# A reordered start for an RMSNorm and projection kernel: other order of loads, two K blocks of weights first, two tiles transposed by DMA

## Chip, cores, metric

One core of a Trainium2 chip. The metric is the device time of one execution in microseconds, median of several; the profile gives a span some 2 us shorter.

## The reference, cut

```python
# x [8, 1024, 768] f32, gamma [768], w_qkv [768, 2304] f32 -> out [8, 1024, 2304] f32
rms = np.sqrt(np.mean(x ** 2, axis=-1, keepdims=True) + eps)
return np.matmul(x / rms * gamma, w_qkv)
```

8192 rows are 64 tiles of 128. K = 768 is six blocks of 128; N = 2304 is four blocks of 512 columns and one of 256. So each tile needs 30 matmuls.

## The kernel before

The weights are loaded in pieces and scaled by gamma into bf16. Rows are normalised last: the eviction multiplies by 1/rms. While the weights arrive, six tiles are worked on at once by a written plan of times (the **head**); 58 tiles follow by a formula. The times only sort the instructions. Each engine then runs its own in order.

```python
ARRIVALS = "xxxwwwxwwwwwxxwww"      # order of the loads on the SP queue
PIECES = [(0, 1, 0, 512), ..., (0, 6, 2048, 256)]   # K blocks k0..k1, columns n0..n0+n
HEAD_PLAN = [(4.41, "trA", 0), (4.45, "stat", 0), ..., (8.02, "mm", 0, 0, "0"), ...]
# [cut] tr: transposes on TensorE; cp: copy PSUM -> SBUF; conv: scaling of a weight block
    def trans_dma(t):
        XT[t] = xTp.tile([P, KO, P], bf16, name="xT")
        nc.sync.dma_start_transpose(out=XT[t], in_=XB[t])
# [cut] idle: matmuls on zeros, meant to keep the TensorE clock up
    def idle(n):
        wps = psum.tile([P, P], f32, name="pm")
        for _ in range(n):
            nc.tensor.matmul(out=wps, lhsT=warm, rhs=warm, start=True, stop=True)
# [cut] after the head
    for t in range(HEAD, MT):
        at(now - 15, load_x, t)
        at(now - 8.5, cast, t)
        at(now - 7.5, trans_dma, t)
        at(now - 5, stat, t)
        at(now - 3, recip, t)
        for n0 in range(0, N, NT):
            at(now, mm, t, n0, range(KO))
            now += min(NT, N - n0) * US
            flip ^= 1
            evac_at(now + 0.2, t, n0, "DVE" if flip else "ACT", gap=1.2)
```

All loads, stores and DMA transposes go through the SP queue, at most eight in flight.

## Time and profile before

| | before |
|---|---|
| device time, median (runs) | 389.93 us (3) |
| span of the profile | 387.9 us |
| TensorE busy | 98% |
| first matmul | 8.48 us |
| first matmul of tile 7 | 51.56 us |
| last matmul ends | 384.35 us |

Columns: start us, us, what.

```profile
384.35 0.02 issue
384.37 0.47 ACT ot L232
```

From 384.35 to 387.9 are 3.55 us of last eviction, last store and program end.

### The profile page before, as it was taken

The page shows a single profiled execution, that of the slowest core. Times are in us where ns is not written, and L with a number is a line of the kernel's source. Part 1 is how long each engine was busy: PE and PEld are TensorE (multiplying, and loading weights), DVE is VectorE, ACT ScalarE, POOL GpSimd, SP SyncE. Part 2 cuts the span into 40 slices and gives each one's busy share as a digit, 9 for nine tenths or more (in the row PEclk, how much of TensorE's full clock was granted, in tenths as well). Part 3 has the DMA queues.
Part 4 walks back from the last instruction along what each step waited for, and adds up shares of the span by engine and source line. Part 5 has one row for each costly group of instructions (what it writes and reads, how often), then busy time and mean ns, then how long its engine had stood idle before and what let it go on. Part 6 is the DMA issues. An engine that isn't in the chain of part 4 may idle for free.

```text
span 387.9 us, 5500 instructions
## 1 busy us (share of the span) xinstructions
PE 379.5 (98%) x1953; PEld 194.3 (50%) x1992; DVE 159.1 (41%) x317; ACT 178.1 (46%) x359; POOL 5.9 (2%) x12
## 2 busy tenths in 40 slices
PE   7999999999999999999999999999999999999996
PEld 6444644554554554554554554554554554554553
DVE  3667634343433343433343433343334343334332
ACT  6652234544444544444534444534434535434532
POOL 1310000000000000000000000000000000000000
PEclk9999999999999999999999999999999999999999
DMA  7999999999999999999999999999999999999974
GB/s 272 392 384 358 308 369 284 397 301 274 333 311 305 279 326 295 290 330 300 276 346 288 302 317 280 318 311 304 287 318 301 297 318 303 287 325 292 292 264 189
DMA packets 87606, 119.51 MB, mean 308 GB/s; under 512 B 50710, under 2 KB 59676, under 8 KB 87580
## 3 DMA queue, kind: packets, MB, share of 16 engines
q1 hardware_dynamic: 87568, 119.17, 100.7%
q8 instruction: 15, 0.25, 0.3%
q14 instruction: 11, 0.09, 0.1%
q10 hardware_dynamic: 12, 0.00, 0.0%
HBM read 32.25 MB, written 75.50 MB: 278 GB/s over the span
## 4 chain that ended last, share of the span: by engine, by line
PE 94%; DMA 3%; SPq 1%; issue 1%; DVE 0%; ACT 0%
PE pm L216 94%; DMA w_f<-in_w_qkv_dram 2%; DMA xT<-xb 2%; SPq L140 0%; SPq L145 0%; PE pm L183 0%; DVE w_b L151 0%; ACT ot L232 0%; DVE ot L230 0%
## 5 line engine op out<-in xcount | busy, mean ns | idle before, releaser
L216 PE MATMUL pm<-w_b,xT 128*128 128x512 bf16 (+1 forms) x1881 | 372.4, 357 | 3.0 <-DMA xT<-xb 0.4
L216 PEld LDWEIGHTS <-xT 128*128 128x128 bf16 x1920 | 187.6, 98 | 186.6 <-issue 0.8
L230 DVE TENSOR_SCALAR ot<-pm,rstd 128x512 f32<-128x512 f32 (+1 forms) x168 | 116.7, 696 | 210.3 <-PE pm L216 210.3
L232 ACT ACTIVATE ot<-pm,rstd 128x512 f32<-128x512 f32 (+1 forms) x152 | 97.9, 645 | 187.0 <-PE pm L216 141.7
L170 ACT ACTIVATE sq<-x_t 128x768 bf16<-128x768 f32 x64 | 53.4, 834 | 10.2 <-DMA x_t<-in_x_dram 10.2
L159 DVE CAST xb<-x_t 128x768 bf16<-128x768 f32 x61 | 33.2, 545 | 4.1 <-DMA x_t<-in_x_dram 4.0
L172 ACT ACTIVATE rms<-ssq,eps_sb 128x1 f32<-128x1 f32 x64 | 18.8, 294 | 2.1
L170 ACT ACTIVATION_READ_ACCUMULATOR sq<-x_t 128x1 f32 x64 | 12.2, 191 | 0.0
L177 DVE RECIPROCAL rstd<-rms 128x1 f32<-128x1 f32 x64 | 9.8, 153 | 0.0
L151 DVE TENSOR_SCALAR w_b<-w_f,g_sb 128x512 bf16<-128x512 f32 (+1 forms) x14 | 6.5, 494 | 6.1 <-DMA w_f<-in_w_qkv_dram 6.0
L153 ACT ACTIVATE w_b<-w_f,g_sb 128x512 bf16<-128x512 f32 (+1 forms) x10 | 6.1, 651 | 5.7 <-DMA w_f<-in_w_qkv_dram 5.7
L155 POOL TENSOR_SCALAR w_b<-w_f,g_sb 128x512 bf16<-128x512 f32 (+1 forms) x6 | 5.2, 864 | 23.5 <-DMA w_f<-in_w_qkv_dram 23.5
L265 PE MATMUL pm<-warm 128*128 128x128 bf16 x35 | 3.8, 300 | 1.0 <-DVE eps_sb L124 1.0
L265 PEld LDWEIGHTS <-warm 128*128 128x128 bf16 x35 | 3.5, 142 | 1.0 <-DVE eps_sb L124 1.0
L197 PE MATMUL pm<-ident_f,x_t 128*128 128x128 f32 x18 | 2.8, 292 | 0.8 <-DMA x_t<-in_x_dram 0.8
L197 PEld LDWEIGHTS pm<-ident_f,x_t 128*128 128x128 f32 x18 | 2.2, 155 | 1.1 <-DMA x_t<-in_x_dram 1.0
L127 ACT ACT_TABLE_LOAD x1 | 1.3, 1283 | 1.3 <-PEq L325 1.3
L159 DVE CAST xT<-pm 128x512 bf16<-128x512 f32 (+1 forms) x3 | 1.7, 596 | 0.0
L159 DVE COPY xT<-pm 128x768 bf16<-128x768 bf16 x3 | 1.6, 547 | 0.0
L248 DVE COPY g_sb<-pm 128x6 f32<-128x6 f32 x1 | 0.2, 165 | 3.6 <-PE pm L247 3.6
L183 PEld LDWEIGHTS <-xb 128*128 128x128 bf16 x18 | 1.2, 98 | 0.9 <-DVE xb L159 0.6
L183 PE MATMUL pm<-ident,xb 128*128 128x128 bf16 x18 | 1.5, 220 | 0.0
(13 smaller groups left out, 3.1 us busy)
## 6 DMA issues: line engine op xcount, KB each, us to landing
out_dram<-ot SPq DMA_DIRECT2D x126, 512.0 KB, 4.0
x_t<-in_x_dram SPq DMA_DIRECT2D x64, 384.0 KB, 4.3
out_dram<-ot SPq DMA_DIRECT2D x64, 128.0 KB, 3.2
w_f<-in_w_qkv_dram SPq DMA_DIRECT2D x2, 1536.0 KB, 13.3
w_f<-in_w_qkv_dram SPq DMA_DIRECT2D x3, 768.0 KB, 8.5
w_f<-in_w_qkv_dram SPq DMA_DIRECT2D x6, 256.0 KB, 5.8
out_dram<-ot SPq DMA_DIRECT2D x4, 256.0 KB, 2.0
xT<-xb SPq DMA_TRANSPOSE x58, 4.4
```

Of the source, the lines that this page charges most:

```text
L151: nc.vector.tensor_scalar(out=o, in0=i, scalar1=g, scalar2=None, op0=mult)
L153: nc.scalar.activation(out=o, in_=i, func=AF.Copy, scale=g, bias=0.0)
L155: nc.gpsimd.tensor_scalar(out=o, in0=i, scalar1=g, scalar2=1.0, op0=mult, op1=mult)
L159: nc.vector.tensor_copy(out=out, in_=in_)
L170: nc.scalar.activation(out=sq, in_=X[t], func=AF.Square, accum_out=ssq)
L172: nc.scalar.activation(out=rms, in_=ssq, func=AF.Sqrt, scale=inv_k, bias=eps_sb)
L177: nc.vector.reciprocal(out=r, in_=RS[t])
L197: nc.tensor.transpose(out=PT[t, h][:, ko - k0, :], in_=X[t][:, ko * P:(ko + 1) * P], identity=ident_f)
L216: nc.tensor.matmul(out=PM[t, n0][:, :nl], lhsT=XT[t][:, ko, :], rhs=w_b[:, ko, n0:n0 + nl], start=(b == 1), stop=(b == KO))
L230: nc.vector.tensor_scalar(out=o, in0=pm[:, :nl], scalar1=RS[t], scalar2=None, op0=mult)
L232: nc.scalar.activation(out=o, in_=pm[:, :nl], func=AF.Copy, scale=RS[t], bias=0.0)
L265: nc.tensor.matmul(out=wps, lhsT=warm, rhs=warm, start=True, stop=True)
```

## The change

The intent: start with two K blocks of weights, order the head by a list schedule chosen for late landings, and take the transposes of tiles 4 and 5 off TensorE.

```diff
-ARRIVALS = "xxxwwwxwwwwwxxwww"
-PIECES = [(0, 1, 0, 512), (1, 2, 0, 512), ...]
+PIECES = [(0, 2, 0, 512), (2, 3, 0, 512), ..., (0, 3, 1024, 512), (3, 6, 1024, 512), ...]
+LOADS = [
+    (-9.00, "w", 0), (-8.99, "x", 0), (-8.98, "x", 1), (-8.97, "x", 2), (-8.96, "w", 1),
     ...
+    (16.69, "t", 4), (16.70, "w", 9), (21.71, "t", 5), (21.72, "w", 10), (21.73, "w", 11),
+    (21.74, "x", 6), (21.75, "x", 7),
+]
 HEAD_PLAN = [   # all times and the order are new
 ...
-    at(0.0, idle, 30)
+    at(0.0, idle, 18)
+    at(2.8, gamma_in)
+    at(2.81, idle, 28)
 ...
-            evac_at(time, *args, gap=1.0)
+            evac_at(time, *args, gap=max(1.0, LOADS[-1][0] + 0.1 - time))
 ...
     for t in range(HEAD, MT):
-        at(now - 15, load_x, t)
-        at(now - 8.5, cast, t)
-        at(now - 7.5, trans_dma, t)
+        ahead = 6.0 if t < HEAD + 5 else 0.0
+        if ("x", t) not in {q[1:] for q in LOADS}:
+            at(now - 15 - ahead, load_x, t)
+        at(now - 8.5 - ahead, cast, t)
+        at(now - 7.5 - ahead, xbar, t)
```

Cut: more buffers (10, 6 and 11 for x, its bf16 copy and its transpose, before 8, 4 and 9), and at most four for each form of weight piece. The stores of the head now wait behind the last loads.

## The prediction

> **What bounds the kernel now.** I read the page first, then the chain of waits, then the waits of TensorE alone, then the timeline of the first 60 us.
>
> ```profile
> PE 379.5 (98%) x1953; PEld 194.3 (50%) x1992; DVE 159.1 (41%) x317; ACT 178.1 (46%) x359; POOL 5.9 (2%) x12
> ...
> PE 94%; DMA 3%; SPq 1%; issue 1%; DVE 0%; ACT 0%
> ```
>
> TensorE is busy for 98% of the span, and 94% of the chain that ended last is its matmuls. What is left to win is the start, before the first matmul, and the holes after it. The waits of TensorE in the whole run, after the opening:
>
> ```profile
> PE pm L216 <- DMA xT<-xb: 0.4, 1, 0.4
> PE pm L216 <- POOL w_b L155: 0.4, 1, 0.4
> PE pm L216 <- DVE w_b L151: 0.2, 1, 0.2
> ```
>
> Columns: total us, times, longest. About 1 us of waits in 388. Now the chain from 4 to 62 us (start us, us, what):
>
> ```profile
> 10.64 0.50 DVE w_b L151
> 11.14 0.04 issue
> 11.19 6.80 PE pm L216 x30
> 17.99 0.34 PE pm L183 x6
> 18.32 0.26 PE pm L216
> 18.58 0.05 issue
> 18.63 0.38 PE pm L216
> 19.01 0.34 PE pm L183 x6
> ...
> 45.30 0.02 issue
> 45.33 0.15 DVE ot L230
> 45.48 6.04 DMA xT<-xb
> 51.52 0.05 issue
> 51.56 6.22 PE pm L216 x31
> ```
>
> The reader is to see three things. The head (six row tiles while the weights arrive) ends at 45.3. Each TensorE transpose of a tile costs 0.34 us in it. Tile 7 waits at 51.56 for its crossbar transpose, issued only at 45.48 because the DMA queue stood behind stores. From 51.56 the matmuls run to 384.35: 57 tiles (7 to 63) in 332.8 us, 5.838 us a tile.
>
> So the head before is: first matmul at 8.48 (timeline), 6 x 5.838 = 35.03 of matmuls, 3 x 0.34 = 1.02 of transposes (tiles 3, 4, 5), 0.43 of holes between 8.48 and 11.19 (2.71 less nine matmuls at 0.216 and one transpose). Sum 44.96; the trace says 45.30, so 0.34 is small change that I carry over as 0.3.
>
> **What the Trainium skill says.** (1) "TensorE: Matmul & The Clock Gate", part 1: a warm matmul of N columns takes N / 2.4 GHz plus some 2.5 ns, 215.7 ns for 512. A tile is 24 of 512 and 6 of 256 columns: 24 x 0.2157 + 6 x 0.109 = 5.83 us. The trace agrees with 5.838: no matmul can be made faster here. (2) "DMA: Bandwidth & Descriptors", on why a semaphore goes up by 16: a transfer has landed only when the last of its 16 engines has. (3) "Runtime: NRT & Kernel Launch", instruction fetch mechanics: instructions come in blocks of 16 KiB (256 instructions) over a DMA, mostly hidden. Together they matter. DMA of 17.5 to 18.6 us:
>
> ```profile
> q1 hardware_dynamic: 206, 0.42, 103.1%
> q8 instruction: 1, 0.02, 6.2%
> ```
>
> 6.2% of 16 engines over 1.1 us is 1.1 us of one engine, on which every later piece queues. The piece behind it (the first six-block one, 7.08 MB into the stream) is due at 22.1 by the rate below and was seen at 23.18:
>
> ```profile
> 23.18 0.88 DVE L151 TENSOR_SCALAR w_b<-w_f,g_sb 128x512 bf16<-128x512 f32 x2 [1.88 <-DMA w_f<-in_w_qkv_dram]
> ```
>
> So the trace shows a fetch that is not hidden when loads are late. (4) "PSUM — Partial Sum Buffer", four rules: eight banks, one output at most one bank. The kernel has all eight in one ring, so an eviction may be late by up to seven outputs.
>
> **The change part by part.** Landing line, from the trace: 2.62 MB were in at 10.64, 5.11 MB at 17.03, 0.39 MB/us; other amounts by that line. An x tile is 0.393 MB, a K block of 512 columns 0.262.
>
> *The start.* The two-block piece goes first, so the third x tile has 1.70 MB ahead of and in it instead of 1.18, and lands at 8.3 (before, 1.70 MB was the second weight piece, used at 8.32) against 6.9. In the new TensorE order all six transposes of tile 2 stand before the first matmul. Six took 0.88. First matmul at 9.2 against 8.48: **+0.7**. In return four matmuls are ready at once; the next piece (1.97 MB, 9.0, plus a scaling of 0.49) is ready at 9.5 when they end at 10.06. Following the order to the fourth tile (48 matmuls, one transpose) I find no hole: pieces due at 11.3, 12.0, 14.0, 16.0 are scaled 0.4 us or more before use. The holes of 0.43 are gone: **-0.4**.
>
> *Transposes.* Tiles 4 and 5 leave TensorE: 2 x 0.34 = **-0.7**.
>
> Head without stalls: 9.2 + 35.03 + 0.34 + 0.3 = 44.9, against 45.3.
>
> *New waits.* After 48 matmuls TensorE is at 9.2 + 10.36 + 0.34 = 19.9 and wants the piece at 5.90 MB, due at 19.05, scaled by 19.55. But the change runs 49 idle matmuls instead of 35 and leaves out 12 transposes before this point: the fetch comes after about as many instructions, now some 33 matmuls into the head (16.8) and not 41 (18.5). It then hits this piece: 20.15, scaled 20.65, a stall of 0.7. Sixteen matmuls on (23.4, or 24.1) comes tile 4, which wants its crossbar transpose. That stands in the queue behind the x tile at 7.08 MB (22.1, or 23.2 with the late engine); its 768 packets of 256 B took 0.8 to 2.2 us in the undisturbed transposes of the trace. It lands at 23.3 to 25. Stall 0 to 1. I put the two stalls at **+0.9** together (0.1 without the fetch, 1.7 at worst). Head end 45.8.
>
> *Tiles 6 and 7.* Their loads now come before all stores and their casts and transposes 6 us earlier. The wait at 51.56 goes: **-0.4**. Against it, stores of the head start about 6 us later and pile up. Until tile 8's transpose (wanted near 57) the queue must move about 17.8 MB at 0.4 MB/us and five transposes: near 56.5. A wait of some tenths is possible: **+0.1**.
>
> Sum: +0.7 - 0.4 - 0.7 + 0.9 - 0.4 + 0.1 = +0.2, less rounding. From 389.93: **390.0 us**. The other 56 tiles and the end don't change.
>
> **Rivals.** *A: the stalls don't come* (the fetch falls elsewhere, the crossbar transpose is quick). For it: the list schedule puts tile 4 just after that landing, and was made for late landings. Then head end 44.9 to 45.0 and no wait at tile 7: 389.1. *B: VectorE blocks.* The cast of tile 6 is placed by a fixed formula before the evictions of tile 5, and its x lands only behind the last weights, at about 34. VectorE stands still for 3 to 4 us there, and again at the casts of tiles 8 to 10. For it: the engine is in order. Against: the eviction held up (tile 5, first column block) is done by 35.7 and its bank is wanted eight outputs later, at about 37. If x is 2 us later, TensorE stalls too: 391 to 392. *C: the delayed stores starve tiles 8 to 10* of transposes: up to 1 us each, 391 to 392. *D: hidden anyway*: the head is bound by arrivals, so that the order doesn't matter. Against: nearly all of TensorE's head from 11.19 is gapless, so removed transposes do count.
>
> **Range and chances.** A gives 389.1, the sum 390.0, B or C 391 to 392; I give A 30%, the sum half, B and C together 20%. Range 389.1 to 391.2. Two per cent is 7.8 us: more than the whole of holes, transposes and start that can be won after the first x tile (1.0 + 1.0 + some 4), and a loss of that size needs B and C several times over. Same 0.985, slower 0.01, faster 0.005.
>
> **What would show it.** First matmul at 9.2 (8.5 would be a win I don't expect). Six transposes on the bf16 transpose line instead of 18, none between 17.9 and 19.4. Two waits of TensorE near 20 and 24, the first on a scaled weight, the second on a crossbar transpose; the instruction block in the DMA view near 17. End of the head at 45.8. No wait at tile 7. VectorE idle for 3 us or more before the cast of tile 6, without a wait of TensorE behind it. The prediction is wrong if TensorE has waits on evictions, or waits of over 1 us on transposes after tile 6, or if the first matmul is before 8.7.

## The result and the profile after

| | before | after |
|---|---|---|
| device time, median (4 runs each) | 390.01 us | 389.32 us |
| span of the profile | 387.9 us | 387.4 us |
| first matmul | 8.48 us | 8.71 us |
| last matmul ends | 384.35 us | 383.38 us |
| last matmul to end of span | 3.55 us | 4.0 us |

The ratio is 0.9984, interval 0.9966 to 1.0001. A ratio is the mean of one kernel's runs over the mean of the other's in the same rounds, so it is not quite the ratio of these medians. The forecast of 390.0 with a range of 389.1 to 391.2 held, and so did "same".

The waits of TensorE after the change (total us, times, longest); apart from those of the opening there is this one:

```profile
PE pm L229 <- DVE w_b L164: 0.6, 1, 0.6
```

The chain in order of time:

```profile
19.56 0.02 issue
19.59 0.50 DVE w_b L164
20.08 0.04 issue
20.12 363.25 PE pm L229 x1872
383.38 0.02 issue
383.40 0.47 ACT ot L245
```

The reader is to see that from 20.12 on TensorE never stops: no wait for tile 4's transpose, none at tile 7. At the steady rate the head then ends at 20.12 + 96 x 0.2158 + 36 x 0.109 = 44.8. The trace's last matmul is 0.97 us earlier, the span only 0.5.

The timeline around the one wait, and the DMA view of 14.5 to 15.5 us:

```profile
17.54 0.56 DVE L172 CAST xb<-x_t 128x768 bf16<-128x768 f32 x1 [1.39 <-DMA x_t<-in_x_dram]
19.59 0.88 DVE L164 TENSOR_SCALAR w_b<-w_f,g_sb 128x512 bf16<-128x512 f32 x2 [0.59 <-DMA w_f<-in_w_qkv_dram]
```

```profile
q1 hardware_dynamic: 152, 0.38, 98.7%
q8 instruction: 1, 0.02, 6.8%
```

One instruction block, 6.8% of 16 engines over 1.0 us: 1.09 us of one engine. It came at 14.6 us, not at 16.8. The x tile after it and the weight piece after that, the one I named, are late. (In five later profiles it is the piece before; see below.)

Why the start cost less than the forecast 0.7 us is in the stretches of 5 to 6.5 and 6.5 to 18 us (last column GB/s), first before, then after:

```profile
5.00:6.50 1.50, 1.14 (x9) 0.88 (x9) 1.35 (x4) 0.48 (x2) 0.00 (x0) 1.00 0.87 247
6.50:18.00 11.50, 10.46 (x59) 5.21 (x61) 6.52 (x16) 7.76 (x17) 3.56 (x4) 1.00 1.04 388
```

```profile
5.00:6.50 1.50, 1.50 (x19) 1.50 (x17) 0.48 (x1) 1.28 (x2) 0.00 (x0) 1.00 1.05 412
6.50:18.00 11.50, 11.38 (x67) 6.03 (x66) 6.85 (x16) 8.64 (x20) 3.33 (x4) 1.00 1.04 390
```

The DMA had a slow stretch when the first weights came. With the weights first, it falls earlier, into the ramp (205 and 279 GB/s in the half microseconds from 2.5 and 3.0, where before had 406). By 8 us, 2.15 MB were moved and not 1.99, which is 0.4 us. A second pair of profiles has the same slow stretches (249 GB/s, and 176 and 299). That the first weight rows are slow is my reading of their packets; no run isolates it.

### The profile page after: what moved, and what is told of

Its sections match the earlier page's. It is cut to its first block, busy times and chain, and to the rows that moved or that the text cites. A ratio compares the mean times of both kernels' runs of the same rounds, so it can differ in the third digit from the quotient of the medians.

```text
span 387.4 us, 5550 instructions
## 1 busy us (share of the span) xinstructions
PE 381.7 (99%) x1994; PEld 195.0 (50%) x1994; DVE 153.7 (40%) x309; ACT 181.2 (47%) x362; POOL 7.5 (2%) x15
## 4 chain that ended last, share of the span: by engine, by line
PE 94%; DMA 4%; SPq 0%; DVE 0%; ACT 0%; issue 0%
PE pm L229 94%; DMA w_f<-in_w_qkv_dram 4%; SPq L153 0%; DVE w_b L164 0%; ACT ot L245 0%; SPq L158 0%
## 5 line engine op out<-in xcount | busy, mean ns | idle before, releaser
L243 DVE TENSOR_SCALAR ot<-pm,rstd 128x512 f32<-128x512 f32 (+1 forms) x165 | 113.6, 693 | 201.0 <-PE pm L229 200.7
L245 ACT ACTIVATE ot<-pm,rstd 128x512 f32<-128x512 f32 (+1 forms) x155 | 100.2, 648 | 190.6 <-PE pm L229 143.9
L185 ACT ACTIVATE rms<-ssq,eps_sb 128x1 f32<-128x1 f32 x64 | 18.9, 295 | 2.1
L168 POOL TENSOR_SCALAR w_b<-w_f,g_sb 128x512 bf16<-128x512 f32 (+1 forms) x9 | 6.8, 765 | 24.3 <-DMA w_f<-in_w_qkv_dram 16.2
L164 DVE TENSOR_SCALAR w_b<-w_f,g_sb 128x512 bf16<-128x512 f32 (+1 forms) x12 | 5.2, 449 | 3.9 <-DMA w_f<-in_w_qkv_dram 3.9
L278 PE MATMUL pm<-warm 128*128 128x128 bf16 x49 | 5.4, 301 | 1.0 <-DVE eps_sb L137 1.0
L278 PEld LDWEIGHTS <-warm 128*128 128x128 bf16 x49 | 4.9, 142 | 1.0 <-DVE eps_sb L137 1.0
L174 ACT CAST xT<-pm 128x256 bf16<-128x256 f32 (+1 forms) x3 | 1.2, 445 | 0.3 <-PE pm L210 0.2
L174 ACT COPY xT<-pm 128x768 bf16<-128x768 bf16 x1 | 0.8, 799 | 0.3 <-PE pm L196 0.3
L196 PEld LDWEIGHTS <-xb 128*128 128x128 bf16 x6 | 0.4, 98 | 0.2
```

The costliest lines, as they stand in the source:

```text
L164: nc.vector.tensor_scalar(out=o, in0=i, scalar1=g, scalar2=None, op0=mult)
L168: nc.gpsimd.tensor_scalar(out=o, in0=i, scalar1=g, scalar2=1.0, op0=mult, op1=mult)
L185: nc.scalar.activation(out=rms, in_=ssq, func=AF.Sqrt, scale=inv_k, bias=eps_sb)
L243: nc.vector.tensor_scalar(out=o, in0=pm[:, :nl], scalar1=RS[t], scalar2=None, op0=mult)
L245: nc.scalar.activation(out=o, in_=pm[:, :nl], func=AF.Copy, scale=RS[t], bias=0.0)
```

## The experiments

Theory: the gain is the transposes taken off TensorE (P), plus the wait before tile 7 taken away by early loads (T), less a wait that TensorE's own instruction fetch makes (F). Rivals: the transposes were hidden (H); the late piece is late for the queue's order (Q); the wait at tile 7 was no matter of the queue (N).

Runs of one series share the runs of the kernel before. Its medians were 390.53 (11 runs), 389.81 (9), 389.95 (9) and 390.25 (9) in the four series; compare within a series.

### The changed kernel again (series 1)

> The changed kernel again, as the yardstick of this series. Every theory: first matmul 8.7 us, one wait of 0.5 to 0.6 us for a scaled weight near 20.1, no wait for a transpose, last matmul at 383.4, time 0.6 to 0.8 us under the kernel before. The time from the last matmul to the end of the span was 3.5 before and 4.0 after in the first profiles: if that is the end of the program as such it is again 4.0, if it is chance it differs.

Median 389.39 (5 runs), ratio 0.9971, interval 0.9959 to 0.9983. Waits of 0.5 and 0.2 for scaled weights, last matmul at 383.50, again 4.0 us to the end of the span. The block hit one piece earlier here:

```profile
16.84 0.98 POOL L168 TENSOR_SCALAR w_b<-w_f,g_sb 128x512 bf16<-128x512 f32 x1 [1.66 <-DMA w_f<-in_w_qkv_dram]
```

That piece was used at 15.72 in the first profile. So which piece is late varies with the moment, and a loss stays: 0.56 there, 0.69 here. The longer end is no chance.

Four more profiles below keep the 49 narrow idle matmuls (both with transposes put back, the one without early loads, the one with more slots). In all four the waits are where they are here, at 17.2 to 17.4 and 17.8 to 18.0; with this one they add up to 0.30 to 0.75 us.

### Wide idle matmuls (series 1)

```diff
-    at(0.0, idle, 18)
+    at(0.0, idle, 4)       # each 512 columns wide, not 128
-    at(2.81, idle, 28)
+    at(2.81, idle, 6)
-    (7.26, "idle", 3)
+    (7.26, "idle", 1)
```

> The 49 narrow idle matmuls become 11 of 512 columns: about the same time, 76 instructions fewer on TensorE. Theory F (TensorE's instruction block of 16 KB is fetched after a count of instructions and holds up one DMA engine, and through it the piece wanted at 19.6): the fetch moves from about 14.9 us to about 22.6 to 23, the first piece of the third column block is used at 18.7 and not 19.59, the 0.56 us wait goes, last matmul near 382.8, time 0.5 us under the changed kernel. Rival Q (the piece is late for the order of the queue or the rate of the memory): it is used at 19.5 to 19.6 as before and the wait stays.

Median 389.23 (5), ratio 0.9966, interval 0.9954 to 0.9978. The block of 14.6 us is gone from its place and stands in the DMA view of 23 to 24 us; the piece is used at 18.51, and no wait is left in the head:

```profile
q8 instruction: 1, 0.02, 6.6%
```

```profile
18.51 0.88 DVE L164 TENSOR_SCALAR w_b<-w_f,g_sb 128x512 bf16<-128x512 f32 x2 [0.57 <-DMA w_f<-in_w_qkv_dram]
```

F holds, Q falls: the queue's order is the same, only the count of TensorE instructions is not. In thirteen of the fourteen profiles the first block came after 204 to 218 TensorE instructions, at times from 14.3 to 24.0 us; in the next run it came after 186. But the last matmul, at 383.28, was not near 382.8. A new wait took the gain:

```profile
68.64 1.90 SPq L219 DMA_TRANSPOSE xT<-xb  x1
73.84 1.47 PE L229 MATMUL pm<-w_b,xT 128*128 128x512 bf16 x6 [0.62 <-DMA xT<-xb]
```

This is tile 11, the first whose transpose isn't early. I had not foreseen it. In the changed kernel this transpose landed at 73.42 and TensorE reached tile 11 at 73.95. Here TensorE was there at 73.2, and the transpose landed at 73.79, 0.37 later: the faster head makes part of the wait, the later landing the rest.

### Fewer wide idle matmuls taken away (series 1): a test that missed

```diff
-    at(0.0, idle, 18)
+    at(0.0, idle, 5)       # 512 columns
-    at(2.81, idle, 28)
+    at(2.81, idle, 11)
```

> 17 wide idle matmuls, 64 instructions fewer than the changed kernel. Theory F: the fetch falls at about 21 us, onto the last x tile or the crossbar transpose of tile 4 behind it; the weight piece is on time (18.7), the wait near 20 goes, and in its place TensorE waits 0.3 to 0.8 us for the transpose of tile 4 near 23; time as the changed kernel within 0.3 us. Rival Q: the wait near 20 stays at 0.5 to 0.6, none near 23.

Median 389.92 (6), ratio 0.9986. My count of idle time was wrong: the 11 took 4.22 us, TensorE began its transposes at 7.8 and the first matmul came at 9.94. The fetch fell at 20.4 and made the last x tile of the head 1 us late, as F says (22.48, against 21.53 in the run before). But TensorE, 1.2 us behind, didn't have to wait for anything. So the wait for tile 4's transpose that I expected was not tested. What follows is something else: a start 1.2 us later moved the last matmul by 0.5 only (383.89), because it swallowed the waits.

### Transposes of tiles 4 and 5 back on TensorE (series 1 and 2)

```diff
-    (16.69, "t", 4), ... (21.71, "t", 5),
+    (22.82, "tr", 4), (22.83, "cp", 4, "DVE"), (22.84, "mm", 4, 0, "012345"),
+    (28.43, "tr", 5), (28.44, "cp", 5, "DVE"), (28.45, "mm", 5, 0, "012345"),
```

> Tiles 4 and 5 are transposed by TensorE again, right before their first matmul, and not by the crossbar; all else as in the changed kernel. Theory P (TensorE's head is gapless there, so its transposes are paid in full): 2 x 0.34 us, plus up to 0.3 us for the copy to SBUF that the matmuls then wait for; last matmul at 384.1 to 384.6, time 0.7 to 1.2 us over the changed kernel. Rival H (the head is bound by arrivals, the transposes were hidden): within 0.2 us of the changed kernel.

Median 391.56 (5), ratio 1.0025; last matmul at 385.83, 2.3 us later than the changed kernel of this series. More than half of it is my placement: TensorE waited 1.3 us for the two copies.

```profile
PE pm L229 <- DVE xT L172: 1.3, 2, 0.7
```

So I placed them better:

```diff
+    (21.95, "tr", 4), (21.96, "cp", 4, "DVE"), (21.97, "mm", 0, 1024, "34"), (21.97, "cast", 5, "DVE"),
+    (27.13, "tr", 5), (27.14, "cp", 5, "DVE"), (27.15, "mm", 3, 1024, "345"),
```

> Tiles 4 and 5 transposed by TensorE again, each transpose now placed ahead of matmuls that don't need it, so that the copy is hidden (in the last run TensorE waited 0.65 us twice for the copy). Theory P (transposes in TensorE's head are paid in full): 2 x 0.34 = 0.7 us over the changed kernel, last matmul at 384.0 to 384.3. Rival H (hidden behind arrivals): last matmul at 383.3 to 383.6.

Median 389.69 (5), ratio 0.9992. The copies are hidden; the chain has the transposes in TensorE's gapless stretch:

```profile
17.80 5.12 PE pm L229 x23
22.92 0.34 PE pm L196 x6
23.25 5.18 PE pm L229 x24
28.43 0.34 PE pm L196 x6
28.77 355.32 PE pm L229 x1836
```

Last matmul at 384.09, 0.6 to 0.7 later than the two profiles of the changed kernel. P holds, H falls: 0.34 each, paid in full; where the copy wasn't covered, in the run before, each wait of TensorE came on top (0.65 on average).

### The kernel before, profiled again (series 2)

No edit.

> The kernel before as a run of its own, for a second profile: in the last series its times spread over 2 us (389.3 to 391.3), those of the changed kernel over 0.5. Theory L (it has waits for crossbar transposes and late pieces whose length is chance): the profile shows waits of TensorE of 0.8 us or more, with the one before tile 7 of another length than 0.44. Rival: the waits are the same to 0.1 us and the spread lies outside the core's span.

Median 389.76 (5). Its chain:

```profile
19.56 25.88 PE pm L216 x138
45.44 5.92 DMA xT<-xb
```

Tile 7 begins at 51.40; tile 6 would end at 45.44 + 5.84 = 51.28. The wait is 0.12 here and was 0.44: chance sets its length. The first matmul waited 0.8 for GpSimd and not 0.4. The end is 3.55 again. The spread of 2 us that the kernel before had in series 1 I didn't catch in a profile; it lies within the span (387.5 to 388.7 us for two of those runs), and its cause stays open.

### Without the early loads, and the early loads alone (series 2)

```diff
-    (21.74, "x", 6), (21.75, "x", 7),
-        ahead = 6.0 if t < HEAD + 5 else 0.0
+        ahead = 0.0
```

> The changed kernel with the loads, casts and transposes of tiles 6 to 10 at their old times. Theory T (the early ones took away the wait before tile 7): TensorE waits for a transpose at tile 6 or 7 again, 0.3 to 1.2 us in all, last matmul at 383.8 to 384.6. Rival N (the wait at tile 7 was not from the order of the queue): no such wait, last matmul at 383.4.

Median 394.65 (4), ratio 1.0123, interval 1.0106 to 1.0141: far more than either theory said.

```profile
PE pm L228 <- DMA xT<-xb: 3.9, 1, 3.9
```

```profile
50.00:55.00 5.00, 1.14 (x9) 0.62 (x8) 1.61 (x3) 1.92 (x4) 0.00 (x0) 1.00 1.09 312
55.00:60.00 5.00, 5.00 (x17) 1.94 (x16) 0.70 (x2) 0.69 (x1) 0.00 (x0) 0.66 1.08 320
```

In the second line the clock column (last but two) falls to 0.66 after TensorE stood still for 3.9 us; the trace has half speed from 55.10 to 58.52. That costs another 5 x 0.34 = 1.7 us. The Trainium skill has this in "TensorE: Matmul & The Clock Gate", part 1 (the clock halves after an idle window of some 3.4 us); the trace agrees. So T holds with a turn: in the changed kernel the early loads are not only worth 0.4. They pay for the stores that were moved behind the loads.

Then the kernel before, with the early part alone:

```diff
+        ahead = 6.0 if t < HEAD + 5 else 0.0
-        at(now - 15, load_x, t)
+        at(-7.2 + 0.01 * t if t < HEAD + 2 else now - 15 - ahead, load_x, t)
         # cast and transpose ahead too; more buffers
```

> The kernel before, with only the early loads, casts and transposes of tiles 6 to 10 and the buffers for them. Theory T: no wait before tile 7, 0.4 us gained or somewhat more, last matmul at 383.8 to 384.0, and a smaller spread of the times. Rival N: the wait stays or turns up at a later tile, last matmul at 384.3 or later.

Median 389.39 (5), ratio 0.9986, interval 0.9973 to 0.9998. No wait from 19.64 to the end, last matmul at 384.03 against 384.19 and 384.35. N falls. By the last matmul the early part is worth 0.16 to 0.32 of the 0.97; counted from the last transpose of the head, which ended at 19.64 here and at 19.56 and 19.34 in the two profiles of before, 0.24 to 0.62.

### The end, and a version that beats both (series 3 and 4)

In the expectations that follow, the end "after the last written byte" is counted from a time set 0.24 us late: 1.14, 1.40 and 1.59 there are 1.38, 1.63 and 1.83 on the clock of the span. The 2.8 to 3.0 and 2.4 from last matmul to last byte hold the same 0.24. Differences aren't touched by it. SP waits at the end for each of its eight slots in turn, and the changed kernel has three DMAs more. With the order of the kernel before, the slot of the last store is the last one waited for. In the changed kernel it is among the first: SP sees this store at 385.95, and the waits for the other slots that follow last until 386.56, though those stores are long done. That is 0.6 us in all five profiles of this order.

```diff
+        if 40 <= t < 45:      # two halves: five DMAs more, last store in the old slot
+            nc.sync.dma_start(out=X[t][:, :K // 2], in_=xf[t * P:(t + 1) * P, :K // 2])
+            nc.sync.dma_start(out=X[t][:, K // 2:], in_=xf[t * P:(t + 1) * P, K // 2:])
```

> The changed kernel; the loads of five tiles in the middle (40 to 44) are each split into two halves, so that the last store lands in the same of the eight semaphore slots as in the kernel before. Theory E (the end after the last written byte depends on the slot: 1.14 us in three profiles with the kernel-before order, 1.58 to 1.59 in five with the changed one, 1.39 to 1.41 in the two between): the end is 1.14 again, last matmul as in the changed kernel (383.4 to 383.5), time 0.45 us under it, 1.0 to 1.4 us under the kernel before. Rival: the end stays at 1.6, it belongs to something else of the change.

Median 389.55 (5), ratio 0.9988: no gain. The end after the last byte did fall, to 1.32. But the last byte came 2.75 us after the last matmul and not 2.16, so that the whole was 4.1. The DMA view of 385.2 to 386.2 shows why; the kernels before and after have no block there:

```profile
q14 instruction: 1, 0.01, 3.0%
```

It is SP's own block, 8 KB, by the count: in all fourteen profiles a block comes after 593 to 597 SP instructions, as one does after 208 to 213, 339 to 341 and 465 to 469. The extra issues bring this count forward, onto the last store. So the slot does what I said, and my remedy undid it.

The next has wide idles, these five halves and the early part for all tiles:

```diff
+        ahead = 6.0
```

> Wide idle matmuls (no wait near 20), the early casts and transposes for all tiles and not up to 10 only (no wait at tile 11, where the wide idles had 0.6), and the slots. If the three theories add up: no wait of TensorE after the first matmul, last matmul at 382.7 to 382.8, end 1.14, time 0.9 to 1.1 us under the changed kernel. If the wait at tile 11 was not from its later transpose, a wait of 0.5 us or more turns up at some tile again.

Median 388.44 (5), ratio 0.9960, interval 0.9947 to 0.9973. No wait of TensorE after its first matmul, last one at 382.65; the end 3.9. The wait at tile 11 was from its later transpose.

On top of that, I moved the first two matmuls ahead of the third tile's transposes:

```diff
-    (7.26, "idle", 1), (7.38, "recip", 0), (7.54, "cpA", 0, "DVE"), ... (8.59, "mm", 0, 0, "01"),
+    (6.90, "cpA", 0, "DVE"), (7.30, "mm", 0, 0, "01"), ... (10.50, "recip", 0),
     # statistics of tiles 0 and 3 and their reciprocals later as well
```

> As the run before it, and the first two matmuls stand before the transposes of the third tile; the copy of the first tile and the copies of the second no longer wait behind the statistics of the first. Theory S (TensorE has a hole of 0.3 us there that idle matmuls fill): first matmul at 7.7 and not 8.5, last matmul 0.3 us earlier, 382.4 to 382.5. Rival A (the next weights are then not there): the 0.3 come back as waits for scaled weights before 20 us, last matmul as in the run before.

Median 388.47 (5), ratio 0.9964. First matmul at 7.71, last at 382.78: nothing gained. S falls. TensorE has holes of 0.2 us at 9.5 and 10.1, for a scaled weight and for the copy of the third tile, and that x tile came 0.2 us later than in the run before. The list of waits has none for scaled weights, so rival A isn't shown: arrivals fit, but 0.2 us lies within the scatter between runs.

Last, the wide idles, early parts for all tiles, and the slot by three SP DMAs fewer:

```diff
+        eng = nc.gpsimd if 40 <= t < 43 else nc.sync
+        eng.dma_start(out=X[t], in_=xf[t * P:(t + 1) * P, :])
```

> As the wide-idle version with early transposes for all tiles, but the last store is brought to the slot of the kernel before by three DMAs fewer on the SP queue (the loads of tiles 40 to 42 go from GpSimd) and not by five more. With five more, SP's own instruction block of 8 KB was fetched just ahead of the last store: last matmul to last written byte 2.8 to 3.0 us and not 2.4. Theory I (slot and block together make the end): no such block before the end, last matmul to end of span 3.5 to 3.6 us, last matmul near 382.7, time 388.0 to 388.3. Rival: the end stays at 3.9 to 4.1, 388.4 to 388.6.

Median 388.15 (5), ratio 0.9946, interval 0.9931 to 0.9960: the fastest of all.

```profile
11.72 370.86 PE pm L230 x1908
382.59 0.02 issue
382.61 0.47 ACT ot L246
```

Span 386.0, so 3.4 us from last matmul to end. TensorE runs from 11.72 to its end without a hole. The margin at the end is thin: SP's block came 0.05 us after the last written byte. Against the changed kernel that is 0.8 us on TensorE and 0.6 at the end by the profiles.

## Why the prediction was right or wrong

| term, us at the last matmul | predicted | first pair of profiles | second pair |
|---|---|---|---|
| first matmul | +0.7 | +0.23 (8.71 - 8.48) | -0.19 (8.54 - 8.73) |
| holes of the head, other than waits named below | -0.4 | -0.62 (0.77 to 0.15) | -0.33 (0.66 to 0.33) |
| transposes off TensorE | -0.7 | -0.68; undone alone: 0.6 to 0.7 | -0.68 |
| new waits | +0.9 | +0.56 | +0.69 |
| wait at tile 7 | -0.4 | -0.44 | -0.12 |
| stores piling up | +0.1 | 0 | 0 |
| sum | +0.2 | -0.95; trace: -0.97 | -0.63; trace: -0.69 |
| end of the program | not looked at | +0.45 | +0.45 |

The second pair is the two kernels profiled again. Single terms differ by up to 0.4 between the pairs, so only what both show is sure.

How the holes are worked out: before, 45.30 - 8.48 less 35.03 of matmuls and 1.02 of transposes; after, 20.12 - 8.71 less 48 x 0.2158, one transpose of 0.34 and the wait of 0.56.

**Right:** three mechanisms. The price of a transpose, the end of the tile 7 wait, and a wait for a scaled weight through the instruction fetch all stand, and experiments that undo or move each one alone confirm them. VectorE stood still before the casts of tiles 6, 8, 9 and 10, about as said in rival B, 2.3 to 4.0 us each (2.7 at tile 6), and no wait of TensorE followed: the eight banks took it up. Rival D fell with the transposes put back.

**Misplaced:** the fetch. I put it at 16.8, 33 matmuls into the head; it came at 14.3 to 14.6, after 25 to 27. Some 1.5 us of this are the matmuls, the rest is the earlier start. (My text also leaves out 12 transposes before the fetch, while the 33 rests on six: in the kernel before, tile 5's came only after it.) The wait of 0.7 that I forecast was 0.30 to 0.75 in six profiles, but on the piece that I named in one of them only; in five it was on the piece before.

**Mis-sized, first:** "First matmul at 9.2 against 8.48: +0.7". I took the landing from the old order by bytes. But the old order has a slow stretch at 5 to 6.5 us that lies elsewhere in the new one; the third x tile was there by 8.0, not 8.3. And the six transposes held up the matmul by 0.69, not 0.88, since the busy time of a row includes the overlap with the next one. Over all profiles nothing sure is left of the term: the first matmul was at 8.48, 8.71 and 8.73 with the old start and at 8.45 to 8.88 in six with the new one, on average 8.64 for both. I had written that a first matmul before 8.7 would show the prediction wrong: it was 8.71 in the first profile, and before 8.7 in three of the five others.

**Mis-sized, second:** "I put the two stalls at +0.9 together". Only one came. Tile 4's transpose was in at about 23.3 (an estimate: its packets ended at 22.8, and tile 5's landed 0.5 us after its last one), and TensorE was there at 20.12 + 16 x 0.216 = 23.6. It was in time by 0.3. The first stall had made TensorE later; that this alone saved it isn't shown. In the wide-idle runs, where TensorE came to tile 4 earlier but the fetch was out of the way, there was no wait either.

**Not seen:** 0.45 us at the end. It made the sum look better than its terms: TensorE gained 0.97, the clock showed 0.5 to 0.7. Without it the time would have been near 388.9, below the stated 389.1: that the range held is luck. A net of terms that err in both directions can land within its range; the table, not the range, tells what was understood.

## What to carry to other kernels

When one engine is full, add up its head term by term and follow each term to the last instruction: gains in the head were given back at tile 11 (with the wide idles) and at the end of the program, far from the head. What an instruction stream fetches uses the same DMA engines as the data, so the number of instructions before a tight load is part of the schedule. Few wide idle matmuls did the work of many narrow ones: with 11 of them the head's first twelve matmuls took 2.59 us, 0.216 each, the steady rate. Moving stores behind loads needed the next tiles' loads and transposes moved with them; without that the wait of 0.4 came back as 3.9. And one profile of each kernel is not enough for a term of 0.2 us: the first matmul alone scatters by 0.4.

## What the Trainium skill lacked or had wrong

- "Runtime: NRT & Kernel Launch", instruction fetch mechanics, calls the cost of a block mostly hidden. Here one block took 1.0 to 1.1 us of one DMA engine and made what was queued behind it 0.9 to 1.1 us late; with 49, 35, 17 and 11 idle matmuls the first came at 14.3 to 14.6, 18.5 to 18.9, 20.4 and 23.1 to 23.2 us. Moved away, a wait of 0.56 us went.
- The same page doesn't say that such a block can meet the last store: with five DMAs more on the SP queue, a block of 8 KB came 0.8 to 0.9 us before the last written byte, which came 0.4 to 0.6 us later than without (three profiles).
- No page has the end of a program by the semaphore slot of its last DMA: 1.38 us after the last written byte in the order of the kernel before (three profiles), 1.83 in that of the changed one (five), 1.63 to 1.65 between (two), and 1.26 to 1.32 with the old slot restored (four). Most of the difference is SP's waits for the slots after that of the last store, 0.6 us in the changed order; why one of these waits takes 0.4 us and the others 0.07 stays open.
- "DMA: Bandwidth & Descriptors", on the DMA transpose, has no duration for one beside loads. The 768 packets of 256 bytes took 0.7 to 2.5 us in the head of the changed kernel, and the first one held a gap of 0.45 us.
- The same page has nothing on a slow first stretch of a new tensor: 247 GB/s over 5 to 6.5 us before, 205 and 279 from 2.5 to 3.5 us after, each time with the first weights, against 375 to 406 from 2.5 to 5 us before and 393 to 426 from 3.5 to 6.5 us after. The cause is not tested.
